# Linear attention: the decays of all six levels first, then all small products of a head and block in one go on TensorE

## The chip, the cores and the metric

The kernel runs on one core of a Trainium2 chip. The metric is the device time of one execution in microseconds (us). In the traces PE is TensorE (PEld its weight loads), ACT is ScalarE, DVE is VectorE, POOL is GpSimd and SP the engine that issues most DMAs.

## What is computed

Two layers act on 2064 tokens (16 learned ones ahead of 2048) of 1024 channels in float32. Layer 0 is a gated convolution module; the change does not touch it. Layer 1 is gated linear attention with four heads (keys and queries of 128 channels, values of 256), where every channel of a head decays by a gate of its own:

```python
def _gla_chunk_step(S, inp):
    qc, kc, vc, gc = inp
    bc = jnp.cumsum(gc, axis=1)
    o_inter = jnp.einsum('bthd,bhde->bthe', qc * jnp.exp(bc), S)
    diff = bc[:, :, None] - bc[:, None, :]
    decay = jnp.exp(jnp.where(causal[None, :, :, None, None], diff, -jnp.inf))
    att = jnp.einsum('bthd,bshd,btshd->bhts', qc, kc, decay)
    o_intra = jnp.einsum('bhts,bshe->bthe', att, vc)
    S_new = jnp.exp(b_last)[..., None] * S + jnp.einsum(
        'bshd,bshe->bhde', kc * jnp.exp(b_last[:, None] - bc), vc)
    return S_new, o_inter + o_intra
...
    o = o * lax.rsqrt(jnp.mean(o * o, axis=-1, keepdims=True) + RMS_EPS) * norm_g
    return (o * jax.nn.silu(r)) @ w_out
...
        h = layer_norm(DN_ALPHA * h + y, post_ln_g[i], post_ln_b[i])
```

## The kernel before

**Projections.** Layer 1 works on four blocks of 512 tokens (the first has the 16 learned ones besides). In each block `proj_units` projects, for head after head, the keys k, the queries q, the values v in four parts, and two gate tiles r0 and r1. A projection is a run of matmuls into a PSUM tile `pj`, each float32 product made of three passes over high and low parts (`mm3`: lines 105, 106 and 107 of the profile). All `pj` tiles share **three buffers** (the pool at L58): a fourth tile's first matmul waits until one of the three has been read out. Behind the keys comes one matmul z for the decay gates (L619), also into a `pj` tile, read by DVE (L620) and ACT (L621). Keys are read out by ACT at L599, queries at L601, the r tiles by ACT at L603 and DVE at L604. The SBUF tiles r0 and r1 have **one buffer each** (L593), so L603 for one head can only write when the head before has read its r (L777).

**Attention of a head** (`gla_units`, a generator of pieces, advanced by `phase3` in step with the projections of the next head: 2.35 pieces per projection). In order: the decayed keys are transposed on PE (pk, L677) and split by ACT and DVE into a pair k_h, k_l; `state(c)` makes the step of the state S for chunk c, three matmuls into `ds` that need that pair. Attention inside a chunk of 128 tokens is cut into six levels, of 64, 32, 16, 8, 4 and 2 tokens. For each level POOL takes differences of the summed gates b (L703, L704), ACT the exponential (L640), and DVE multiplies by keys and queries (L706, L707): this gives a tile A. Small matmuls multiply parts of A by other parts of it. The levels 64, 32 and 16 go to `att` at once, level by level (L713: 4, 8 and 16 matmuls). The levels 8, 4 and 2, and the products inside pairs (tile A1), go to the two tiles `sm` (L741, L742: 64 matmuls in all) behind the last level. DVE masks and sums them (L744 to L753) into `at`, ACT and POOL split that into a_h and a_l, and PE makes the output o of a chunk out of the states and of these (L105 to L107 again, six matmuls per chunk). Then o is squared (ACT L764), copied to SBUF (`osb`, DVE L765), scaled (DVE L767, POOL L768, DVE L770), transposed back (oT, PE L775) and multiplied by r (og, L777).

**PSUM.** Besides `pj` there are three buffers named g (transposes, `sm`, o, oT, and the transposed tokens of the next block, `trb`), and one each for `att` and `ds`: eight banks, all in use.

**Order.** The program is written as above; a list scheduler with its own timing model then sets the order of the instructions on each engine. So every engine's order is fixed in the program, and an instruction that waits holds up all that stand behind it on its engine.

Of the kernel before, what the change touches and what calls it, by code (L numbers as in the profile page):

```python
# [11 lines left out]
F32 = mybir.dt.float32  # L12
# [5 lines left out]
DRAM = bass.MemoryType.DRAM  # L18

P = 128  # L20
D = 1024
KD = D // P
T = 2064
# [9 lines left out]
ALPHA = math.sqrt(2.0)  # L33
# [15 lines left out]
class Trunk:  # L49
    """Two layers; float32 products as three float32r passes over exact high and low parts."""  # L50
# [34 lines left out]
    def load(self, srcs, nm, eng, parts=((0, KD),)):  # L85
        """[P, k, w] blocks from DRAM as (high, low) pairs per k; in turn with what `parts` yields."""
        out = []
        for i, src in enumerate(srcs):
            nk, w = src.shape[1:]
            r, h, l = (  # L90
                t[:, : nk * w].rearrange("p (k c) -> p k c", c=w)
                for t in (self.raw(f"{nm}_{i}"), *self.pair(f"{nm}_{i}"))
            )
            for k0, k1 in parts:
                ks = slice(k0, min(k1, nk))
                self.nc.sync.dma_start(r[:, ks], src[:, ks])
                self.split(r[:, ks], h[:, ks], l[:, ks], eng)
            out += [(h[:, k], l[:, k]) for k in range(nk)]
        return out

    def mm3(self, out, ops):
        """out = sum over (lhi, llo, rhi, rlo) of lhi*rhi + lhi*rlo + llo*rhi."""
        mm, n = self.nc.tensor.matmul, len(ops)
        for i, (lh, ll, rh, rl) in enumerate(ops):
            mm(out, lhsT=lh, rhs=rh, start=(i == 0), stop=False)  # L105
            mm(out, lhsT=lh, rhs=rl, start=False, stop=False)  # L106
            mm(out, lhsT=ll, rhs=rh, start=False, stop=(i == n - 1))  # L107
# [5 lines left out]

    def phase1(self, x_cm, w1, pp, c_d, sz_d, hook):
        nc = self.nc
# [5 lines left out]
        # what the last convolutions of the second segment use, apart from what closes earlier  # L121
        last = (KD - 1) % 3
# [31 lines left out]
        def first():  # L154
            """parts of the first weights, in turn with the first part of x"""
            load_x(0, (0, 1))
            yield 0, 2
            load_x(0, (1, 2))
            yield 2, 4
            load_x(0, (2, 4))  # L160
            yield 4, KD
# [104 lines left out]
        # the last gates: first the tokens that layer 0's next step starts with  # L266
# [17 lines left out]

    def phase2_open(self, pp, c_d, sz_d):
        """what may start while the last gates are projected"""
        nc = self.nc
        self.c_d, self.sz_d = c_d, sz_d
        self.lp = self.pool(self.st2, name="p2l", bufs=2, side="right")
        self.pm = [self.pool(self.st2, name="p2p", bufs=1, space=PSUM, side="right")]  # L290
        self.st2w = ExitStack()
        self.wrp = self.pool(self.st2w, name="p2r", bufs=WRB, side="right")
        self.prm2 = self.lp.tile([P, 16], F32, name="prm2", bufs=1)
        nc.sync.dma_start(self.prm2, pp)
        self.normed, self.gated, self.nnorm = deque(), deque(), 0
# [70 lines left out]
    def out_tile(self, h, l, w, xt, m, nm):  # L366
        """xt[:m] = ALPHA * xt[:m] + (h + l)^T w"""
        for e in range(2):
            es = slice(512 * e, 512 * (e + 1))
            ps = self.pjt(f"{nm}_{e}")[:m]  # L370
            self.mm3(ps, [(h[:, k], l[:, k], w[k][0][:, es], w[k][1][:, es]) for k in range(KD)])
            self.nc.vector.scalar_tensor_tensor(xt[:m, es], xt[:m, es], ALPHA, ps, op0=ALU.mult, op1=ALU.add)  # L372

    def ln_stats(self, sm, r, n, sfx):
        """mean and 1 / standard deviation (columns 0, 2) of the rows of r [n, D]"""
        nc = self.nc
        st = sm.tile([P, 2, 6], F32, tag="st", name=f"st{sfx}")
        rs = sm.tile([P, 4], F32, tag="rs", name=f"rs{sfx}")
        for i in range(2):
            nc.vector.bn_stats(st[:n, i], r[:n, 512 * i : 512 * (i + 1)])  # L380
        nc.vector.bn_aggr(rs[:n, 0:2], st[:n])
        nc.vector.tensor_scalar(rs[:n, 1:2], rs[:n, 1:2], LN_EPS, None, op0=ALU.add)  # L382
        nc.gpsimd.tensor_tensor(rs[:n, 2:3], rs[:n, 1:2], self.mhalf[:n, 0:1], op=ALU.pow)  # L383
        return rs

    def post_ln(self, sm, r, n, g, b, sfx):
        """LayerNorm over the free axis of r [n, D] (tokens on partitions)."""
# [46 lines left out]

    def phase3_open(self, ws):
        """what may start while layer 0 ends"""
# [15 lines left out]
    def phase3_init(self, wa2, pp, og_d):  # L452
# [11 lines left out]
        # w_a2 at rows 0, 32 (high parts) and 64 (low part)  # L464
# [10 lines left out]
    def block(self, bi):  # L475
        """h1 of a block of tokens, transposed and split; yields before each chunk of tokens"""
# [24 lines left out]
    def gla_consts(self, pool, tmp):  # L501
        nc, K = self.nc, self
        """Masks of the 32x32 diagonal blocks by level, block mask, chunk resets."""
# [13 lines left out]
        for lev, m in enumerate((8, 4, 2, 1, 0)):  # L517
            f = full
            nc.gpsimd.memset(f, 1.0)
            if m:  # L520
# [3 lines left out]
                # s (partition) in the first half of segment, t in the second half  # L524
# [6 lines left out]
            # the blocks on the diagonal, gathered into 32 columns  # L531
# [18 lines left out]
    def proj_units(self):  # L550
        """yields after each unit of PE work; weights of the next tile are loaded one tile ahead"""
# [3 lines left out]
        for i, (bi, (kind, h, _, wd)) in enumerate(jobs):  # L555
# [3 lines left out]
            # the meta tokens have no outputs: only keys, gates and values of theirs are needed  # L559
# [71 lines left out]
    def pair3(self, nm, x, eng, sfx, bufs=2):  # L631
        """x [P, 4, P] as (high, low)"""
        h, l = (self.gp.tile([P, 4, P], F32R, tag=f"{nm}_{i}", name=f"{nm}_{i}{sfx}", bufs=bufs) for i in "hl")
        self.split(x, h, l, eng)
        return h, l

    def gla_units(self, h, hd, bi, t0, n):
# [4 lines left out]
        if off:  # L642
            # meta tokens only enter the state
# [16 lines left out]
        # decays from and to the chunk's ends  # L660
# [17 lines left out]
        kth, ktl = self.pair3("k", pt, nc.vector, nm)  # L678
        Ss = []

        def state(c):
            """the state before chunk c, and its step"""
# [7 lines left out]
            self.mm3(ds, [(kth[:, c], ktl[:, c], vh[:, c], vl[:, c])])  # L690
# [3 lines left out]
        att = self.pa.tile([P, 4, P], F32, tag="att", name=f"att{nm}")  # L694
        nc.vector.memset(att, 0.0)
        lv = {}
        for m in (64, 32, 16, 8, 4, 2):
            A = self.gp.tile([P, 512], F32, tag="A", name=f"A{nm}_{m}", bufs=4)
            view = lambda x: x.rearrange("p (s u i) -> p s u i", u=2, i=m)
            Av, bv, kv, qv = view(A), view(bs), view(ks), view(qs)  # L700
            nsg = 512 // (2 * m)
            mid = bv[:, :, 0, m - 1 : m].to_broadcast([P, nsg, m])
# [6 lines left out]
            if m >= 16:  # L709
                for c in range(4):  # L710
                    for s in range(0, P, 2 * m):
                        a = c * P + s
                        nc.tensor.matmul(  # L713
                            att[s : s + m, c, s + m : s + 2 * m],
                            lhsT=A[:, a : a + m],
                            rhs=A[:, a + m : a + 2 * m],
                            start=False,
                            stop=False,
                            skip_group_check=True,
                        )  # L720
                state(len(Ss))
                yield
        # by blocks of 32: queries of odd rows, decayed to the row before, then all queries
# [6 lines left out]
        nc.gpsimd.tensor_copy(A1[:, :, 16:], qs.rearrange("p (a t) -> p a t", t=32))  # L730
        state(3)
        yield
        red = self.gp.tile([P, 4, 32], F32, tag="red", name=f"red{nm}")
        for c2 in range(2):
            sm = self.pt.tile([P, 2, 144], F32, tag="g", name=f"sm{nm}_{c2}")
            for c in range(2):
                for s in range(0, P, 32):
                    a = (2 * c2 + c) * P + s
                    w = slice(a, a + 32)
                    for i, m in enumerate((8, 4, 2)):  # L740
                        nc.tensor.matmul(sm[s : s + 32, c, 48 + 32 * i : 80 + 32 * i], lhsT=lv[m][:, w], rhs=lv[m][:, w], start=True, stop=True, skip_group_check=True)  # L741
                    nc.tensor.matmul(sm[s : s + 32, c, :48], lhsT=ks[:, w], rhs=A1[:, a // 32], start=True, stop=True, skip_group_check=True)  # L742
# [41 lines left out]
    def phase3(self, wo):  # L784
        """returns what is left of the last head, and half of layer 1's out-projection"""
# [20 lines left out]
    def load_half(self, wo, e, staging=None):  # L806
        """yields before each of four tiles"""
# [11 lines left out]

    def phase4(self, wo, rows, out):  # L820
# [3 lines left out]
        # the pair that the last projection reads, and the two others  # L824
# [114 lines left out]
```

## Time and profile before

| what | value |
|---|---|
| time, median of three runs (least, most) | 1764.78 us (1763.5, 1766.14) |
| span of the profiled execution | 1762.7 us |
| PE busy in it | 1705.0 us, 97% |
| PE weight loads | 1522.8 us, 86% |
| DVE, ACT, POOL busy | 79%, 48%, 53% |
| layer 1 without its out-projection, 829 to 1600 us: PE busy | 746.13 of 771 us |

The profiled execution's span lies 2.1 us under the median of the runs: that is what lies around the span. Busy PE is the total over the whole kernel; both layers are included. Names in the trace leave out numbers, in the order of a program they stand: `pj_b1k2_0` is the projection of block 1, keys, head 2; `o1_0_1` is block 1, head 0, second half of the tokens.

### The profile page before, as it was taken

To read this page: it belongs to the slowest core of one execution; us is meant where nothing else is said; L and a number is where in the kernel's file an instruction comes from. 1 tells how busy PE (TensorE), PEld (TensorE's weight loads), DVE (VectorE), ACT (ScalarE), POOL (GpSimd) and SP (SyncE) were. 2 spreads that over 40 slices of the span, in tenths; PEclk is the share of its full clock that TensorE was granted. 3 is DMA by queue.
4 is the path that set the end of the run, shared out by engine and by line. 5 is a ranking of instruction groups with operands and counts; after the bars stand their busy time and mean duration, and the time that the engine had idled before them with its cause. 6 is when DMAs were issued, how large, how long until landed. Compare 5 with 4: busy or idle time off the path is not lost.

```text
span 1762.7 us, 30279 instructions
## 1 busy us (share of the span) xinstructions
PE 1705.0 (97%) x12291; PEld 1522.8 (86%) x12291; DVE 1397.2 (79%) x1900; ACT 848.2 (48%) x1308; POOL 934.3 (53%) x675
## 2 busy tenths in 40 slices
PE   8999999999998999998999999999999999999998
PEld 8999999999997777777888888888888878888886
DVE  5799999999988888877676687787878697777665
ACT  6455565655635344445455454555555455541000
POOL 1889999999966687756233133333334153331000
PEclk9999999999998999999999999999999999999999
DMA  6111111211256444433113222232223322344441
GB/s 243 37 49 36 47 51 37 73 57 53 92 182 219 132 158 153 143 111 105 64 61 108 86 97 81 77 112 71 86 83 94 112 73 85 120 159 164 149 136 62
DMA packets 102492, 178.80 MB, mean 101 GB/s; under 512 B 8736, under 2 KB 64672, under 8 KB 102352
## 3 DMA queue, kind: packets, MB, share of 16 engines
q1 hardware_dynamic: 102352, 176.87, 30.4%
q8 instruction: 96, 1.57, 0.4%
q14 instruction: 44, 0.36, 0.1%
HBM read 134.70 MB, written 42.14 MB: 100 GB/s over the span
## 4 chain that ended last, share of the span: by engine, by line
PE 72%; DVE 14%; ACT 5%; POOL 4%; DMA 2%; issue 2%; SPq 0%; DVEq 0%; POOLq 0%; ACTq 0%
PE pj_y L107 5%; PE pj_y L106 5%; PE pj_y L105 5%; PE pj_g L106 3%; PE pj_g L107 3%; PE pj_a L106 3%; PE pj_z L106 3%; PE pj_z L107 3%; PE pj_z L105 3%; PE pj_a L105 3%; PE pj_g L105 3%; PE pj_a L107 3%; DVE A L707 2%; DVE A L706 2%; DMA c<-c_d 1%
## 5 line engine op out<-in xcount | busy, mean ns | idle before, releaser
L194 POOL TENSOR_TENSOR gacc<-gacc,prod 128x1024 f32<-128x1024 f32 (+1 forms) x156 | 384.5, 2468 | 60.1 <-ACT prod L193 51.2
L202 DVE SCALAR_TENSOR_TENSOR cacc<-glu,prm,cacc 128x1024 f32<-128x1024 f32 (+1 forms) x292 | 374.8, 1294 | 6.8
L703 POOL TENSOR_TENSOR A<-b 128x256 f32<-128x256 f32 x96 | 77.7, 809 | 304.8 <-DVE b L629 136.8
L193 ACT ACTIVATE prod<-glu,prm 128x1024 f32<-128x1024 f32 (+1 forms) x156 | 178.6, 1154 | 82.9 <-POOL gacc L194 82.7
L105 PE MATMUL pj_g<-xh,h_w 128*128 128x344 f32 x384 | 124.6, 324 | 5.3 <-ACT h_w L72 4.4
L106 PE MATMUL pj_g<-xl,h_w 128*128 128x344 f32 x384 | 124.6, 325 | 0.3 <-DVE xl L73 0.3
L107 PE MATMUL pj_g<-xh,l_w 128*128 128x344 f32 x384 | 123.7, 323 | 0.0
L106 PE MATMUL pj_a<-xl,h_w 128*128 128x344 f32 x384 | 123.1, 321 | 0.0
L105 PE MATMUL pj_z<-xh,h_w 128*128 128x344 f32 x384 | 123.1, 321 | 0.0
L106 PE MATMUL pj_z<-xl,h_w 128*128 128x344 f32 x384 | 123.0, 320 | 0.0
L105 PE MATMUL pj_a<-xh,h_w 128*128 128x344 f32 x384 | 123.0, 320 | 0.0
L107 PE MATMUL pj_z<-xh,l_w 128*128 128x344 f32 x384 | 122.8, 320 | 0.0
L107 PE MATMUL pj_a<-xh,l_w 128*128 128x344 f32 x384 | 122.7, 320 | 0.0
L106 PE MATMUL pj_y<-wol,h_gt 128*128 128x512 f32 (+1 forms) x272 | 110.2, 406 | 1.0 <-DVE wol L73 1.0
L107 PE MATMUL pj_y<-woh,l_gt 128*128 128x512 f32 (+1 forms) x272 | 109.2, 409 | 1.9 <-DVE l_gt L73 1.9
L105 PE MATMUL pj_y<-woh,h_gt 128*128 128x512 f32 (+1 forms) x272 | 110.8, 411 | 0.0
L105 PE MATMUL pj_y<-w4h,h_g 128*128 128x512 f32 x256 | 99.7, 390 | 0.0
L106 PE MATMUL pj_y<-w4l,h_g 128*128 128x512 f32 x256 | 99.6, 390 | 0.0
L107 PE MATMUL pj_y<-w4h,l_g 128*128 128x512 f32 x256 | 99.5, 389 | 0.0
L640 ACT ACTIVATE A<-A 128x512 f32<-128x512 f32 (+1 forms) x112 | 66.6, 596 | 52.9 <-POOL A L704 52.2
L383 POOL TENSOR_TENSOR rs<-rs,mhalf 128x1 f32<-128x1 f32 x16 | 14.5, 906 | 145.2 <-DVE rs L382 145.2
L372 DVE SCALAR_TENSOR_TENSOR xt<-xt,pj_y 128x512 f32<-128x512 f32 (+1 forms) x66 | 44.7, 680 | 58.8 <-PE pj_y L107 58.8
(420 smaller groups left out, 5474.6 us busy)
## 6 DMA issues: line engine op xcount, KB each, us to landing
r_w<-w SPq DMA_DIRECT2D x24, 512.0 KB, 3.5
sz_d<-sz SPq DMA_DIRECT2D x48, 172.0 KB, 1.9
c<-c_d SPq DMA_DIRECT2D x16, 512.0 KB, 5.1
szb<-sz_d SPq DMA_DIRECT2D x16, 512.0 KB, 5.0
xt<-x_tok SPq DMA_DIRECT2D x16, 512.0 KB, 3.7
h_d<-xt SPq DMA_DIRECT2D x16, 512.0 KB, 2.6
r_h1b<-h_d SPq DMA_DIRECT2D x16, 512.0 KB, 3.6
og_d<-og SPq DMA_DIRECT2D x32, 256.0 KB, 2.8
```

The source lines that it names most:

```text
L105: mm(out, lhsT=lh, rhs=rh, start=(i == 0), stop=False)
L106: mm(out, lhsT=lh, rhs=rl, start=False, stop=False)
L107: mm(out, lhsT=ll, rhs=rh, start=False, stop=(i == n - 1))
L193: nc.scalar.activation(pr, src(k), AF.Copy, scale=tap(k))
L194: nc.gpsimd.tensor_tensor(st["g"], st["g"], pr, op=ALU.add)
L202: nc.vector.scalar_tensor_tensor(out, src(k), tap(k), acc, op0=ALU.mult, op1=ALU.add)
L372: self.nc.vector.scalar_tensor_tensor(xt[:m, es], xt[:m, es], ALPHA, ps, op0=ALU.mult, op1=ALU.add)
L383: nc.gpsimd.tensor_tensor(rs[:n, 2:3], rs[:n, 1:2], self.mhalf[:n, 0:1], op=ALU.pow)
L640: ex = lambda o, i: nc.scalar.activation(o, i, AF.Exp, scale=1.0 / TAU)
L703: nc.gpsimd.tensor_tensor(Av[:, :, 0], mid, bv[:, :, 0], op=ALU.subtract)
L706: nc.vector.tensor_tensor(Av[:, :, 0], Av[:, :, 0], kv[:, :, 0], op=ALU.mult)
L707: nc.vector.tensor_tensor(Av[:, :, 1], Av[:, :, 1], qv[:, :, 1], op=ALU.mult)
```

## The change

Inside `gla_units` the six levels are made first, without any product: POOL, ACT and DVE work as before, in the order 64, 32, 16, 8, 4, 2, then A1. For that the tiles A get six buffers in place of four, and the transposed keys' pair one in place of two. The steps of the state stand between the levels and behind A1. All 92 small products of the head and block then come in one piece, which the scheduler is told to issue only after the last step of the state (`issue_after`): first the 64 products 32 wide, chunk by chunk, then the levels 16, 32 and 64. The piece that masks and sums follows. Nothing is computed otherwise; the rest of the difference is comments taken out, so lines behind stand up to six higher.

```diff
-        kth, ktl = self.pair3("k", pt, nc.vector, nm)
-        Ss = []
+        kth, ktl = self.pair3("k", pt, nc.vector, nm, 1)
+        Ss, steps = [], []
...
-            self.mm3(ds, [(kth[:, c], ktl[:, c], vh[:, c], vl[:, c])])
+            steps.append(self.mm3(ds, [(kth[:, c], ktl[:, c], vh[:, c], vl[:, c])]))
...
-        att = self.pa.tile([P, 4, P], F32, tag="att", name=f"att{nm}")
-        nc.vector.memset(att, 0.0)
-        for m in (64, 32, 16, 8, 4, 2):
-            A = self.gp.tile([P, 512], F32, tag="A", name=f"A{nm}_{m}", bufs=4)
+        def level(m):
+            A = self.gp.tile([P, 512], F32, tag="A", name=f"A{nm}_{m}", bufs=6)
...
+        for i, ms in enumerate(((64, 32), (16, 8), (4, 2))):
+            for m in ms:
+                level(m)
+            if i < 2:
                 state(len(Ss))
                 yield
...
+        state(2)
+        yield
+        att = self.pa.tile([P, 4, P], F32, tag="att", name=f"att{nm}")
+        nc.vector.memset(att, 0.0)
         state(3)
         yield
+        sms = [self.pt.tile([P, 2, 144], F32, tag="g", name=f"sm{nm}_{c2}") for c2 in range(2)]
+        part = partial(nc.tensor.matmul, skip_group_check=True)
+        with self.tc.issue_after(steps[-1].ins):
+            for c in range(4):
+                sm = sms[c // 2][:, c % 2]
+                for s in range(0, P, 32):
+                    w = slice(c * P + s, c * P + s + 32)
+                    part(sm[s : s + 32, :48], lhsT=ks[:, w], rhs=A1[:, (c * P + s) // 32], start=True, stop=True)
+                    for i, m in enumerate((8, 4, 2)):
+                        part(sm[s : s + 32, 48 + 32 * i : 80 + 32 * i], lhsT=lv[m][:, w], rhs=lv[m][:, w], start=True, stop=True)
+            for m in (16, 32, 64):
+                A = lv[m]
+                for c in range(4):
+                    for s in range(0, P, 2 * m):
+                        a = c * P + s
+                        part(att[s : s + m, c, s + m : s + 2 * m], lhsT=A[:, a : a + m], rhs=A[:, a + m : a + 2 * m], start=False, stop=False)
```

The scheduler orders layer 1 anew. Two places show how. The first is PE in block 1, between the end of the projections r of head 1 and the keys and queries of head 2, while the output of head 0 is finished. Before, in PE's order:

```order
L106 MATMUL pj_b1r11_0_10484<-xlb1_8834,h_b1r11_0_10401 128x512
L107 MATMUL pj_b1r11_0_10484<-xhb1_8833,l_b1r11_0_10402 128x512
...
L775 MATMUL oT1_0_1_10365<-ident_73,osb1_0_10228 128x128 x4
L677 MATMUL pk1_1_10447<-ident_73,kh1_1_10438 128x128 x4
L713 MATMUL att1_1_10456<-A1_1_16_10534 16x16 x15
L105 MATMUL pj_b1k2_0_10572<-xhb1_8833,h_b1k2_0_10478 128x512
L106 MATMUL pj_b1k2_0_10572<-xlb1_8834,h_b1k2_0_10478 128x512
```

After, at the same place:

```order
L107 MATMUL pj_b1k2_0_10565<-xhb1_8826,l_b1k2_0_10479 128x512
...
L107 MATMUL o1_0_1_10281<-vhb1v0_9451,a_l1_0_10225 128x256
L620 MATMUL pj_z1_2_0_10703<-ah1_9453,a2_7087 128x512
L105 MATMUL pj_b1q2_0_10738<-xhb1_8826,h_b1q2_0_10559 128x512
L106 MATMUL pj_b1q2_0_10738<-xlb1_8827,h_b1q2_0_10559 128x512
...
L105 MATMUL pj_b1q2_0_10738<-xhb1_8826,h_b1q2_0_10559 128x512
L781 MATMUL oT1_0_0_10330<-ident_73,osb1_0_10228 128x128 x4
L781 MATMUL oT1_0_1_10365<-ident_73,osb1_0_10228 128x128 x4
L678 MATMUL pk1_1_10447<-ident_73,kh1_1_10438 128x128 x4
L106 MATMUL pj_b1q2_0_10738<-xlb1_8827,h_b1q2_0_10559 128x512
```

Before, the transposes oT of head 0 and pk of head 1 stand ahead of the keys of head 2, with small products around them. After, they stand behind the keys, the gate product z and 19 matmuls of the queries of head 2.

The second excerpt is the same place on ACT. Before (L603 reads out r0 and r1 of head 1, L599 the keys of head 2, L621 the gate product):

```order
L603 ACTIVATE b1r01_10406<-pj_b1r01_0_10407 128x512
L72 ACTIVATE k_h1_1_10452<-pk1_1_10447 128x512
L603 ACTIVATE b1r11_10483<-pj_b1r11_0_10484 128x512
L72 ACTIVATE h_b1v2_1_10732<-r_b1v2_1_10731 128x1024
L599 ACTIVATE b1k2_10571<-pj_b1k2_0_10572 128x512
L72 ACTIVATE sh1_1_1_10525<-Sm1_8061 128x256
L621 ACTIVATE b1_2_10669<-pj_z1_2_0_10670,prm3_7082 128x512
```

After (the same are L604, L600 and L622):

```order
L600 ACTIVATE b1k2_10564<-pj_b1k2_0_10565 128x512
...
L641 ACTIVATE kh1_1_10438<-kh1_1_10438 128x512
L622 ACTIVATE b1_2_10702<-pj_z1_2_0_10703,prm3_7082 128x512
L623 ACTIVATE b1_2_10702<-b1_2_10702 128x512
L624 ACT_TABLE_LOAD
L624 ACTIVATE b1_2_10702<-b1_2_10702 128x512
L641 ACT_TABLE_LOAD
L641 ACTIVATE eb1_2_10970<-b1_2_10702 128x512
L604 ACTIVATE b1r01_10406<-pj_b1r01_0_10407 128x512
L72 ACTIVATE k_h1_1_10452<-pk1_1_10447 128x512
L604 ACTIVATE b1r11_10483<-pj_b1r11_0_10484 128x512
```

Before, ACT reads out both r tiles and then the keys. After, it reads out the keys and the gate product first and the r tiles behind them.

The third place is PE at the end of block 1, where the tokens of block 2 are transposed (`trb`) and head 2's output is made. Before:

```order
L107 MATMUL o1_2_1_11336<-vhb1v2_10804,a_l1_2_11315 128x256
L490 MATMUL trb2_256_0_11411<-ident_73,r_h1b2_256_11409 128x128 x4
L106 MATMUL pj_b1v3_3_11511<-l_b1v3_1_11277,xhb1_8833 128x256
L107 MATMUL pj_b1v3_3_11511<-h_b1v3_1_11276,xlb1_8834 128x256
L490 MATMUL trb2_256_1_11418<-ident_73,r_h1b2_256_11409 128x128 x4
L105 MATMUL pj_b1v3_3_11511<-h_b1v3_1_11276,xhb1_8833 128x256
...
L107 MATMUL pj_b1r03_0_11545<-xhb1_8833,l_b1r03_0_11370 128x512
L713 MATMUL att1_3_11634<-A1_3_64_11636 64x64 x2
L775 MATMUL oT1_2_0_11452<-ident_73,osb1_2_11318 128x128 x4
L490 MATMUL trb2_384_0_11462<-ident_73,r_h1b2_384_11460 128x128 x4
```

After:

```order
L746 MATMUL att1_2_11127<-A1_2_64_11026 64x64 x4
L491 MATMUL trb2_0_0_11255<-ident_73,r_h1b2_0_11253 128x128 x4
L491 MATMUL trb2_0_1_11262<-ident_73,r_h1b2_0_11253 128x128 x4
L105 MATMUL o1_2_0_11320<-sh1_2_0_11038,q_h1_2_10979 128x256
...
L107 MATMUL o1_2_1_11336<-sh1_2_2_11085,q_l1_2_10980 128x256
L105 MATMUL o1_2_0_11320<-vhb1v2_10804,a_h1_2_11314 128x256
...
L107 MATMUL o1_2_1_11336<-vhb1v2_10804,a_l1_2_11315 128x256
L491 MATMUL trb2_256_1_11418<-ident_73,r_h1b2_256_11409 128x128 x4
L781 MATMUL oT1_2_0_11452<-ident_73,osb1_2_11318 128x128
L491 MATMUL trb2_384_0_11462<-ident_73,r_h1b2_384_11460 128x128 x4
```

Before, the last o product of head 2 is followed by the rest of v3 and all of r0 of head 3 (24 matmuls), then oT. After, the 92 small products end in front of two transposed tiles and six o products, then come the o products that need a_h; and behind the last o product stand four transposes, then oT.

## Rows read from the trace of the kernel before

**Rows 1.** The page: span, and busy time and instructions of the engines.
```profile
span 1762.7 us, 30279 instructions
PE 1705.0 (97%) x12291; PEld 1522.8 (86%) x12291; DVE 1397.2 (79%) x1900; ACT 848.2 (48%) x1308; POOL 934.3 (53%) x675
```

**Rows 2.** Busy time by stretch, layer 1: us, engines, PEclk, DMA share, GB/s.
```profile
829.00:1600.00 771.00, 746.13 (x6946) 645.67 (x6945) 584.35 (x1025) 393.66 (x723) 262.55 (x284) 0.99 0.28 92
```

**Rows 3.** Timeline, PE: start, us, engine, line, out<-in, count; around one run of sm.
```profile
1245.10 0.28 PE L106 MATMUL ds<-vlb2v,k_h 128*128 128x256 f32 x1
1245.22 0.28 PE L107 MATMUL ds<-vhb2v,k_l 128*128 128x256 f32 x1
1245.43 0.26 PE L741 MATMUL sm<-A 128*32 128x32 f32 x4
...
1247.05 0.25 PE L742 MATMUL sm<-A,b2k 128*32 128x48 f32 x2
1247.23 0.50 PE L106 MATMUL pj_b2q<-xlb,h_b2q 128*128 128x512 f32 x1
1247.57 0.40 PE L107 MATMUL pj_b2q<-xhb,l_b2q 128*128 128x512 f32 x1
1247.81 0.39 PE L105 MATMUL pj_b2q<-xhb,h_b2q 128*128 128x512 f32 x1
```

**Rows 4.** Timeline, PE: the first and the last of 103 runs of small products.
```profile
830.62 0.33 PE L713 MATMUL att<-A 128*64 128x64 f32 x2
...
1585.53 0.25 PE L742 MATMUL sm<-A,b3k 128*32 128x48 f32 x2
```

**Rows 5.** Timeline, all engines: from a last o product to the second r evacuated.
```profile
1082.59 0.28 PE L107 MATMUL o<-vhb1v,a_l 128*128 128x256 f32 x1
...
1083.63 0.68 DVE L765 COPY osb<-o 128x512 f32<-128x512 f32 x1
...
1087.18 1.14 DVE L770 TENSOR_SCALAR osb<-osb,sq 128x256 f32<-128x256 f32 x4
...
1090.31 0.60 PE L677 MATMUL pk<-ident,kh 128*128 128x128 f32 x4
...
1091.74 0.59 ACT L72 ACTIVATE k_h<-pk 128x512 fp32r<-128x512 f32 x1
1091.88 0.74 DVE L777 SCALAR_TENSOR_TENSOR og<-oT,prm,b1r 128x512 f32<-128x512 f32 x1
...
1092.65 0.60 ACT L603 ACTIVATE b1r<-pj_b1r 128x512 f32<-128x512 f32 x1 [0.33 <-DVE og L777]
```

**Rows 6.** Timeline: the last sm product of a head, and its a_h.
```profile
1203.18 0.25 PE L742 MATMUL sm<-A,b1k 128*32 128x48 f32 x2
...
1207.11 0.63 ACT L72 ACTIVATE a_h<-at 128x512 fp32r<-128x512 f32 x1 [0.22 <-DVE at L753]
...
1207.88 1.93 POOL L73 TENSOR_TENSOR a_l<-at,a_h 128x512 fp32r<-128x512 f32 x1 [17.03 <-ACT a_h L72]
```

**Rows 7.** Waits of PE by releaser: us in total, times, longest.
```profile
PE pj_b0q L105 <- ACT b0k L599: 1.0, 1, 1.0
```

**Rows 8.** Timeline: a gate product z and its two readers.
```profile
1051.62 0.50 PE L619 MATMUL pj_z<-ah,a 128*128 128x512 f32 x1
...
1053.43 0.74 DVE L620 TENSOR_SCALAR gl<-pj_z,prm 128x512 f32<-128x512 f32 x1
...
1054.20 0.69 ACT L621 ACTIVATE b<-pj_z,prm 128x512 f32<-128x512 f32 x1 [3.06 <-DVE gl L620]
```

**Rows 9.** Timeline: a wait of PE (in brackets, with its releaser).
```profile
836.13 0.68 PE L677 MATMUL pk<-ident,kh 128*128 128x128 f32 x4 [3.38 <-DVE kh L671]
```

**Rows 10.** Busy time by stretch, behind that wait (columns as rows 2).
```profile
836.70:840.00 3.30, 3.30 (x17) 3.30 (x17) 3.04 (x6) 1.26 (x3) 0.00 (x0) 0.50 0.70 236
840.00:843.00 3.00, 3.00 (x63) 2.49 (x63) 0.48 (x1) 0.82 (x3) 1.19 (x2) 0.99 0.08 33
```

**Rows 11.** The page's costliest groups: first decay difference of a level, on POOL.
```profile
L703 POOL TENSOR_TENSOR A<-b 128x256 f32<-128x256 f32 x96 | 77.7, 809 | 304.8 <-DVE b L629 136.8
```

More of the change, by code (lines that the diff above doesn't have):

```diff
@@ L106, in mm3 @@
             mm(out, lhsT=lh, rhs=rl, start=False, stop=False)
-            mm(out, lhsT=ll, rhs=rh, start=False, stop=(i == n - 1))
+            end = mm(out, lhsT=ll, rhs=rh, start=False, stop=(i == n - 1))
+        return end
     def pjt(self, nm):
@@ L689, in state @@
             ds = self.pa.tile([P, 4, P], F32, tag="ds", name=f"ds{nm}_{c}").rearrange("p a b -> p (a b)")[:, :256]
-            self.mm3(ds, [(kth[:, c], ktl[:, c], vh[:, c], vl[:, c])])
+            steps.append(self.mm3(ds, [(kth[:, c], ktl[:, c], vh[:, c], vl[:, c])]))
             nc.vector.scalar_tensor_tensor(S, S, el[:, c], ds, op0=ALU.mult, op1=ALU.add)
         yield
-        att = self.pa.tile([P, 4, P], F32, tag="att", name=f"att{nm}")
-        nc.vector.memset(att, 0.0)
         lv = {}
-        for m in (64, 32, 16, 8, 4, 2):
-            A = self.gp.tile([P, 512], F32, tag="A", name=f"A{nm}_{m}", bufs=4)
+        def level(m):
+            A = self.gp.tile([P, 512], F32, tag="A", name=f"A{nm}_{m}", bufs=6)
             view = lambda x: x.rearrange("p (s u i) -> p s u i", u=2, i=m)
             Av, bv, kv, qv = view(A), view(bs), view(ks), view(qs)
-            nsg = 512 // (2 * m)
-            mid = bv[:, :, 0, m - 1 : m].to_broadcast([P, nsg, m])
+            mid = bv[:, :, 0, m - 1 : m].to_broadcast([P, 512 // (2 * m), m])
             nc.gpsimd.tensor_tensor(Av[:, :, 0], mid, bv[:, :, 0], op=ALU.subtract)
@@ L708, in gla_units @@
             lv[m] = A
[L709 to L720, printed above, removed]
+        for i, ms in enumerate(((64, 32), (16, 8), (4, 2))):
+            for m in ms:
+                level(m)
+            if i < 2:
                 state(len(Ss))
@@ L730, in gla_units @@
         nc.gpsimd.tensor_copy(A1[:, :, 16:], qs.rearrange("p (a t) -> p a t", t=32))
+        state(2)
+        yield
+        att = self.pa.tile([P, 4, P], F32, tag="att", name=f"att{nm}")
+        nc.vector.memset(att, 0.0)
         state(3)
         yield
-        red = self.gp.tile([P, 4, 32], F32, tag="red", name=f"red{nm}")
[L734 to L742, printed above, removed]
+        sms = [self.pt.tile([P, 2, 144], F32, tag="g", name=f"sm{nm}_{c2}") for c2 in range(2)]
[14 more added lines that the diff above has]
+                        part(att[s : s + m, c, s + m : s + 2 * m], lhsT=A[:, a : a + m], rhs=A[:, a + m : a + 2 * m], start=False, stop=False)
+        red = self.gp.tile([P, 4, 32], F32, tag="red", name=f"red{nm}")
+        for c2, sm in enumerate(sms):
             ms = self.gp.tile([P, 2, 144], F32, tag="ms", name=f"ms{nm}_{c2}")
```

## The prediction, made before the changed kernel ran

> **What bounds the kernel now.** I read the page first: PE is busy 1705.0 of 1762.7 us, and its instructions run in an order that the program fixes [rows 1]. So the time is PE's own work plus its waits, and the change has to be costed in both. Then the stretch that it touches: in layer 1, from 829 to 1600 us, PE is busy 746.13 of 771 us, which leaves 24.9 us without work [rows 2]. Up to there both programs have the same order. The list of PE's waits shows what is short when PE does wait on a projection tile: the queries of block 0 waited 1.0 us once for the keys to be read out of PSUM [rows 7]. The timeline shows in what company the small products run: in **103 runs**, from 830.62 to 1585.53 us, most of them cut into by projections [rows 4]. In the order of the changed program they are 16 runs of 92. So the change does what it says, and "it changes nothing" is no rival.
>
> **1. The switches saved.** Around one run [rows 3]: two full-width matmuls of 256 columns start 0.12 us apart (1245.10, 1245.22), but the first small one comes 0.21 after the second, so going in costs 0.09. The last small matmuls start at 1247.05 (a row of two) and the projection at 1247.23. By the starts of such rows the small ones need about 0.02 each, so some 0.14 of the 0.18 is not work, against 0.02 inside the run: 0.12. The projection's next matmul starts 0.34 later (1247.57) where the one after needs 0.24 (1247.81): 0.10. Together **0.31 us per run**. 103 − 16 = 87 runs fewer make 27.0 us. Against that each of the 16 pieces switches once inside itself, from products 32 wide to wider ones; I take the way in, 0.09, for that: 16 × 0.09 = 1.4. Gain 27.0 − 1.4 = **−26 us**. Bounds: if the way out costs half as much elsewhere, (0.09 + 0.11) × 87 = −18; if the way in also slows the next step by 0.10, as the way out does, 0.41 × 87 = −36.
>
> The Trainium skill, "TensorEngine Tiling (Array Packing)", Key Properties, says that a change of the tiling mode drains TensorE, and gives no price. By that rule the switch inside a piece is a full one, 16 × 0.31 = 5 us, and the gain 22; rows 3 agree that a switch costs something. The sum does not use it.
>
> **2. What the new order puts in front of the r tiles.** This is the term that decides. An r tile leaves its `pj` buffer only when og of the head before has read the old r, since r0 and r1 have one SBUF buffer each. The way there is long: the last o product ends at 1082.87, the copy of o starts at 1083.63, the scaling ends at 1088.32, and the second r is read out at 1092.65 to 1093.25, released by og [rows 5]: 10.4 us. Before, PE's order is r0, r1, oT, pk, then the next keys, and ACT reads out r0, r1, then keys. After, PE's order is r0, r1, keys, the last o products, z, 19 matmuls of the queries, and only then oT. While oT is not done, two of the three `pj` buffers hold r tiles. The keys take the third; z must wait until ACT has read out the keys, and the queries until DVE and ACT have read z. Nothing stands between them on PE but what waits too. What that costs: the keys' read-out, 0 to 1.0 us (1.0 in [rows 7]; the six o products in between, at 0.12, can cover 0.7); z's, from its start at 1051.62 to the end of ACT's read at 1054.89, 3.27 us less the 0.25 that z takes itself, so 3.0 with a loaded DVE [rows 8]; with an idle one 0.50 + 0.1 + 0.74 + 0.69 = 2.0, less 0.25, or somewhat less where matmuls overlap, 1.6. So each place costs 1.6 to 4.0; I take 3.5, near the loaded row, since DVE is behind with levels and splits at that point. Going through the order head by head I count six places of z and queries in front of oT (heads 2 and 3 of blocks 1, 2 and 3) and three of the same kind with other projections (two in block 0, and a tile of the out-projection in front of the oT of block 3's head 2): 9 × 3.5 = **+31 us** (14 to 36).
>
> **3. The ends of blocks 0, 1 and 2.** At these three places the last head's products meet the transposes of the next block, and no projection stands between. From the last 32-wide product (end 1203.43) to a_h (end 1207.74) DVE and ACT need 4.3 us [rows 6]. PE has 28 products of `att` in between (about 1.0 us by the pace of rows 3, 48 products in 1.7), eight transposes at 0.60 per four [rows 5] and six o products of 0.12: 2.7 us, so it waits 1.6. From the last o product to the first scaled part of `osb` it takes 4.6 us, to all four 5.45 [rows 5], and there are four to twelve transposes in front of oT, of which the later ones need a PSUM buffer g that o still holds until its copy is done (1083.63 + 0.68, that is 1.4 us after the last o): 3.5 to 4.4 of wait, and about 1 us each at two transposed tiles. Together 1.6 + 4.4 + 2 = **8 us, three times: +24** (5.4 each without the two waits for g, so 16; 12 each if a_l, 1.93 us of POOL behind a_h in [rows 6], is waited for too, so 36). Before, the rest of v and all of r0, some 8 us of PE work, lay in that gap.
>
> **4. The transposed keys.** In five heads (1_2, 2_0, 2_1, 2_2, 3_0) pk is followed within 0.3 to 0.4 us of PE work by the first step of the state, which needs k_h. From the end of pk (1090.91) to that of k_h (1092.33) it is 1.4 us [rows 5]. Before, 2 to 6 us of projection lay in between. 5 × 1.1 = 5.5, with a queue on ACT now and then **+6** (0 where ACT's other reads also shift the pair earlier, 13 where DVE's k_l is late too). The single buffer of the pair costs nothing: the last step of the state of one head stands long before pk of the next.
>
> **5. The clock.** Behind a wait of 3.38 us [rows 9] the granted clock was 0.50, the lower of the two levels (1.2 GHz), for the stretch from 836.70 to 840.00; behind that it was 0.99 [rows 10]. At half speed 3.3 us hold 1.65 us of work, so such a wait costs 1.65 more. Of the 9 + 6 longer waits above I let ten do that: 10 × 1.65 = **+17** (0 to 20).
>
> The Trainium skill, "TensorE: Matmul & The Clock Gate", HAM oscillation, describes the same: an engine that waits again and again starts cold each time. By that all 15 would pay, +25 in place of +17, and the time would be 1825; rows 9 and 10 show one such case here, and cannot say how many.
>
> **6. The rest.** Levels, exponentials and masks are as many as before, on engines with 47 to 79% of use or less; six buffers of A in place of four hold POOL's next levels back until a piece is done, which is rival C. The `issue_after` itself adds an order on PE, no instruction.
>
> **Sum.** −26 + 31 + 24 + 6 + 17 = +52. Against the profiled span 1762.7 + 52 = 1814.7; the median of the runs lies 2.1 above the span, so **1817 us**. All low ends together (gain 36, then 14, 16, 0, 0) give −6: 1759. All high ends (gain 18, then 36, 36, 13, 20) give +87: 1852.
>
> **Rivals.**
> - **A, faster.** The waits of parts 2 to 4 are hidden and only the switches remain: 1764.8 − 26 = **1739**. The place is z: if ACT read out keys and z as soon as PE ends them, and DVE is idle when z comes, z costs less than 1 us. It decides where all new waits together stay under 26 us, that is 1.6 us per head. For it speaks that the order was made by a scheduler that had these dependencies before it; against it, that the r tiles hold two of three buffers whatever DVE does, and that 3.0 us is the row's duration, of which 1.6 cannot be hidden.
> - **B, it cancels.** Waits at their low ends and no new falls of the clock: −26 + 14 + 16 + 0 = +4, so about **1769** (1760 to 1776).
> - **C, POOL.** In the changed order a_l of a head stands on POOL behind the level work of the next head: twelve differences at 0.81 us [rows 11] and a copy, some 10.5 us, which cannot start before the piece is through, since all six A are in use. If o's products with a_l then wait 3 us in 13 of 16 heads, 39 more: 1817 + 39 = **1856**. Against it: in most heads two or more projections stand between the piece and those products.
>
> **How the numbers follow.** Chances: the forecast (parts 2 to 5 within their bounds, 1776 to 1850) 0.70; B 0.10; A 0.13; C 0.07. A difference of 0.2%, 3.5 us, is about what a measurement of this kernel tells from none. B splits evenly between within 0.2% (up to 1768.3) and slower. So faster 0.13, within 0.2% 0.05, slower 0.70 + 0.07 + 0.05 = 0.82. The range for 8 in 10 leaves out A and half of C and of the lowest part of B: 1764 to 1852.
>
> **What would show it.** Runs: PE's timeline should show 16 pieces; next to a piece the steps 0.21 and 0.34 of rows 3, and nothing of the kind elsewhere. PE's busy time from 829 to the end of layer 1's heads should fall by about 26 us less what the lower clock adds. Part 2: in the list of waits, projections of queries waiting for ACT's or DVE's read of z, and z for ACT's read of the keys, some 30 us where there was 1.0; L604 waiting for og. Part 3: oT waiting for `osb` and o for a_h, 3 times 6 us or more, at the ends of blocks 0, 1, 2. Part 4: ds waiting for k_h. Part 5: stretches of granted clock 0.50 behind these waits. I am wrong if z's readers come at once, or if the pieces themselves run slower than their parts did, since 92 products wait for one another's PSUM tile; then PE's busy time would rise and not its waits.

## The result, and the profile after

The changed kernel takes 1855.46 us (1852.01 to 1857.23, four runs) against 1764.7 before (four runs): a ratio of **1.0512** (95% interval 1.05 to 1.0525), so 90.8 us slower. The sign and most places were forecast; the size, 1817 with a range up to 1852, was too small.

The page after, its span and busy time (against [rows 1]), and the stretch of layer 1 to the end by the windows view (columns as in [rows 2]; the last row is the same stretch of the kernel before):

```profile
span 1855.3 us, 30235 instructions
PE 1729.4 (93%) x12291; PEld 1548.0 (83%) x12291; DVE 1409.3 (76%) x1900; ACT 850.1 (46%) x1308; POOL 913.7 (49%) x675
829.00:1855.30 1026.30, 925.88 (x7637) 799.44 (x7635) 698.95 (x1194) 409.97 (x740) 256.56 (x300) 0.94 0.27 90
829.00:1762.70 933.70, 900.87 (x7637) 773.77 (x7635) 685.09 (x1194) 407.76 (x740) 277.06 (x300) 0.99 0.30 99
```

The 92.6 us by which this execution's span is longer split in three. PE without work: 1026.30 − 925.88 = 100.4 against 32.8, **+67.6**. Half clock: going through the trace, from 829 us to the end of PE's work the granted clock was 0.50 in 17 stretches, 116 us in all, with PE busy for 87.4 of them; before, in three stretches of 3.4 us, with PE busy throughout. Half of 87.4 less half of 10.2 is **+38.6**. The rest is 92.6 − 67.6 − 38.6 = **−13.6**, the switches saved, less small things.

The waits of PE after, by releaser (us in total, times, longest):

```profile
PE oT L781 <- DVE osb L776: 9.8, 5, 3.1
PE o L105 <- DVE xlb L494: 7.9, 3, 3.5
PE pj_z L620 <- ACT b3k L600: 6.6, 2, 5.9
PE pj_z L620 <- ACT b2k L600: 5.9, 2, 5.2
PE trb L491 <- DVE xlb L494: 5.8, 3, 4.6
PE ds L105 <- ACT k_h L72: 5.5, 5, 1.5
PE o L105 <- ACT kh L770: 4.9, 6, 1.8
PE pj_z L620 <- ACT b1k L600: 4.9, 2, 4.2
...
PE pj_b3q L105 <- ACT b L622: 4.1, 2, 2.6
PE pj_b1q L105 <- ACT b L622: 3.8, 2, 2.6
```

Before, z waited for nothing, queries had the one row of [rows 7], and ds did not wait for k_h; the other waits named here had these rows:

```profile
PE oT L775 <- DVE osb L770: 2.5, 4, 1.5
PE o L105 <- DVE xlb L493: 2.1, 1, 2.1
PE trb L490 <- DVE xlb L493: 2.0, 2, 1.0
PE o L105 <- ACT kh L764: 1.5, 2, 0.8
```

Read them by place. z waits for the keys' read-out (L600), queries for z's (L622): part 2. oT for `osb`, and o and trb for a PSUM buffer that token transposes hold (xlb): part 3. ds for k_h: part 4. The row of o for kh (L770) is a wait for the square of the chunk before, which ACT writes into the tile kh; the prediction had no part for it.

One piece of small products, PE's timeline (against [rows 3]): the way in (0.21 between the starts, 0.09 of it extra) and the second step behind (0.22, 0.10 of it extra) cost what they did, and all 92 products, two records each, lie between.

```profile
1304.37 0.28 PE L107 MATMUL ds<-vhb2v,k_l 128*128 128x256 f32 x1
1304.58 0.27 PE L738 MATMUL sm<-A,b2k 128*32 128x48 f32 x2
...
1308.72 0.39 PE L105 MATMUL o<-sh,q_h 128*128 128x256 f32 x1
1308.94 0.28 PE L106 MATMUL o<-sl,q_h 128*128 128x256 f32 x1
1309.06 0.28 PE L107 MATMUL o<-sh,q_l 128*128 128x256 f32 x1
```

The longest kind of wait, at z of the last head of block 2. First ACT's timeline (in brackets the idle time before and who ended it):

```profile
1379.44 1.06 ACT L72 ACTIVATE h_b2v<-r_b2v 128x1024 fp32r<-128x1024 f32 x1 [7.49 <-DMA r_b2v<-wv]
1380.41 0.36 ACT L770 ACTIVATE kh<-o 128x256 f32<-128x256 f32 x1
...
1385.52 1.06 ACT L72 ACTIVATE h_b2v<-r_b2v 128x1024 fp32r<-128x1024 f32 x1 [4.66 <-DMA r_b2v<-wv]
1386.48 0.58 ACT L600 ACTIVATE b2k<-pj_b2k 128x512 f32<-128x512 f32 x1
```

Then SP's queue (the issues of transfers):

```profile
1359.03 0.33 SPq L486 DMA_DIRECT2D r_h1b<-h_d  x1
1374.17 0.33 SPq L96 DMA_DIRECT2D r_b2v<-wv  x1
...
1381.79 0.33 SPq L96 DMA_DIRECT2D r_b2v<-wv  x1
```

And PE:

```profile
1381.61 0.28 PE L107 MATMUL o<-vhb2v,a_l 128*128 128x256 f32 x1
1387.11 0.80 PE L620 MATMUL pj_z<-ah,a 128*128 128x512 f32 x1 [5.23 <-ACT b2k L600]
1387.98 0.58 PE L105 MATMUL o<-sh,q_h 128*128 128x256 f32 x1
...
1390.84 0.80 PE L105 MATMUL pj_b2q<-xhb,h_b2q 128*128 128x512 f32 x1 [1.20 <-ACT b L622]
```

The tokens of the next block (r_h1b) took one of two staging buffers at 1359, and the weights of the values had to share the other: the second half was issued at 1381.79, when DVE had read the first. ACT stood in front of its split for 4.66 us, and **behind it in ACT's queue** stood the read-out of the keys, for which z waited. (The 5.86 us at the last z of block 3 have the same shape: there ACT stood 4.41 us for a weight transfer of the out-projection.) In the stretch that follows, the windows view shows half clock:

```profile
1382.20:1395.80 13.60, 7.41 (x19) 5.54 (x20) 7.15 (x12) 7.87 (x14) 2.05 (x2) 0.50 0.23 77
```

### The profile page after: what moved, and what is told of

It is laid out like the page before. It is cut to its first block, busy times and chain, and to the rows that moved or that the text cites. A ratio compares the mean times of both kernels' runs of the same rounds, so it can differ in the third digit from the quotient of the medians.

```text
span 1855.3 us, 30235 instructions
## 1 busy us (share of the span) xinstructions
PE 1729.4 (93%) x12291; PEld 1548.0 (83%) x12291; DVE 1409.3 (76%) x1900; ACT 850.1 (46%) x1308; POOL 913.7 (49%) x675
## 3 DMA queue, kind: packets, MB, share of 16 engines
q1 hardware_dynamic: 102352, 176.87, 28.2%
## 4 chain that ended last, share of the span: by engine, by line
PE 72%; DVE 12%; POOL 6%; ACT 4%; DMA 4%; issue 3%; SPq 0%; DVEq 0%; ACTq 0%; POOLq 0%
PE pj_y L107 4%; PE pj_y L105 4%; PE pj_y L106 4%; PE pj_g L106 3%; PE pj_a L106 3%; PE pj_g L107 3%; PE pj_z L107 3%; PE pj_z L106 3%; PE pj_a L105 3%; PE pj_a L107 3%; PE pj_z L105 3%; PE pj_g L105 3%; PE sm L740 2%; DMA c<-c_d 1%; DVE A L707 1%
## 5 line engine op out<-in xcount | busy, mean ns | idle before, releaser
L73 POOL TENSOR_TENSOR q_l<-eb,q_h 128x512 fp32r<-128x512 f32 x16 | 21.5, 1347 | 172.6 <-ACT q_h L72 172.6
```

The lines of the kernel that those rows point to most:

```text
L73: eng.tensor_tensor(lo, raw, hi, op=ALU.subtract)
```

## The experiments

Theory P is the prediction's part 2 (r tiles hold two of three projection buffers until og of the head before). Theory W came out of the rows above (a late weight transfer holds up ACT's queue). e1 to e11 are one run each and are compared with the run of the kernel before beside them, 1763.6 to 1767.8 us. Every edit lets the scheduler order layer 1 anew, so a run shows what an edit does together with its new order.

**e1, two buffers for r** (and the room for them).

```diff
-                t = hd[kind] = self.hp.tile([P, BMAX], F32, tag=kind, name=f"{nm}", bufs=2 if kind in "kq" else 1)
+                t = hd[kind] = self.hp.tile([P, BMAX], F32, tag=kind, name=f"{nm}", bufs=2)
```

> The changed kernel with two SBUF buffers for each of the tiles r0 and r1 (room from tiles that one engine alone uses, and from tokens of blocks 1 and 3). Theory P (projection tiles r hold two of three PSUM buffers until og of the head before): r can be read out at once, so z and the queries find a free buffer. In the profile of the changed kernel PE waits 20 us at z for the keys' or r's read-out and 10 us at queries for z's; both should fall under 5 in all, with some 15 us of the half clock behind them: 1855 - 25 - 15 = about 1815. Rival W (ACT stands at a weight split whose transfer is late, and the keys' read-out stands behind it): the r tiles are read out on the same ACT, so at least the three longest waits, 15 us, stay: about 1840.

Measured 1816.41. All waits of z and of queries for z's readers are gone from the list, whose head is now

```profile
PE oT L781 <- DVE osb L776: 14.2, 7, 3.5
PE o L105 <- ACT kh L770: 7.5, 10, 1.4
PE o L105 <- ACT a_h L72: 7.1, 3, 3.4
```

So P holds, the longest waits included: with a third `pj` buffer free, a late read-out of the keys stops nothing. oT does not stand earlier in e1's order (in block 1 it stands behind z and most or all of the queries, at two heads behind most of the values as well), so it is the second r buffer and not an earlier oT that frees z. PE's time without work fell by 23.8 us, and what the half clock takes by 10.8.

**e2, z in another PSUM bank.**

```diff
-  ps = self.pjt(f"z{bi}_{h}_{c0}")[:, :m]
+  ps = self.pa.tile([P, 4, P], F32, tag="att", name=f"z{bi}_{h}_{c0}").rearrange("p a b -> p (a b)")[:, :m]
```

> The changed kernel with the gate product z in the PSUM bank of att instead of one of the three projection buffers. Theory P: z waits for nothing of the projections, and queries only for the keys' read-out: the 10 us of queries that wait for z go, and of z's 20 us most: about 1820. Rival W: the keys' read-out is late by itself, so the three longest waits (4.2, 5.2, 5.9 us) move from z to the queries; only the 10 us go, and about 5 us of clock: about 1840.

Measured 1865.31: slower, against both. The waits moved: queries wait for the keys' read-out, and oT, in the new order, for `osb`:

```profile
PE oT L781 <- DVE osb L776: 36.4, 8, 8.8
PE pj_b2q L105 <- ACT b2k L600: 12.7, 3, 4.5
PE pj_b1q L105 <- ACT b1k L600: 8.0, 2, 4.1
```

With two r tiles in PSUM the queries are short of a buffer as z was; but the scheduler made another order, so the run tells nothing about sizes, and neither forecast can be weighed by it.

**e3, the tokens in a buffer of their own** (with the same room made), and **e4, e2 and e3 together.**

```diff
-  h1 = self.raw(f"h1{nm}_{o}")[:, :D]
+  h1 = self.hp.tile([P, D], F32, tag="h1", name=f"r_h1{nm}_{o}", bufs=1) if bi else self.raw(f"h1{nm}_{o}")[:, :D]
```

> The changed kernel with a buffer of its own for the tokens of the next block, so that both staging buffers stay with the weights. Theory P: no change at z and at the queries, 1850 to 1857. Rival W: the transfer of the values' second half is issued one split earlier; the three waits of 4.2 to 5.9 us at z fall to about 1 us, and the half clock behind them: 1855 - 12 - 8 = about 1835.

> The changed kernel with z in att's bank and the tokens in a buffer of their own. If P and W are both at work, what e2 and e3 give adds up: about 1815. If P alone, as e2; if W alone, as e3.

Measured 1827.93 and 1867.51. e3: z's waits for the keys of blocks 1 and 2 fell from 4.9 and 5.9 to 1.5 and 1.4 us, for block 3, where no tokens follow, 6.6 became 6.7. The rows of e3:

```profile
PE pj_z L620 <- ACT b3k L600: 6.7, 3, 4.5
PE pj_z L620 <- ACT b1k L600: 1.5, 2, 0.8
PE pj_z L620 <- ACT b2k L600: 1.4, 2, 0.7
```

W is at work in two of three places. The whole gain, 27.5 us, is more than these 7.9 us and their clock, so part of it comes from elsewhere in the new order. e4 takes what e2 takes, and nothing adds up.

**e8, control: the room alone.** Tiles that only DVE touches (`ms`, `red`), and the learned tokens' values, with one buffer; token tiles of 512 columns for blocks 1 and 3.

> Control for e1 and e3: the changed kernel with only the room made that they need (one buffer in place of two for tiles that DVE alone uses and for the learned tokens' values, smaller token tiles for blocks 1 and 3), and nothing put into it. If e1 and e3 owe their times to the second r buffer and to the tokens' own buffer, this is 1850 to 1862; if to the new order that the scheduler makes of any edit, it is as much faster as they, 1815 to 1830.

Measured 1856.65: e1 and e3 owe their times to the buffers, with the orders that these allow, and not to the room made for them.

**e5, not held back; e6, held back to the first step** (the two pieces of the diff)**; e7, the kernel before with its 64 products 32 wide in one piece behind `issue_after(steps[-1].ins)`.**

```diff
-        with self.tc.issue_after(steps[-1].ins):
+        if True:
...
-        with self.tc.issue_after(steps[-1].ins):
+        with self.tc.issue_after(steps[0].ins):
```

> The changed kernel without the order that holds the 92 products back until the last step of the state: the levels are still made first and the products still written in one piece, but the scheduler places them when their levels are ready (59 runs in its order, none behind the last step by rule). Theory L (the harm comes from holding the products back: everything behind them, from the masks to oT, starts late and oT is late for the r tiles): the waits of PE in layer 1 come back to 25 to 35 us, few falls of the clock, and the gain of 44 runs fewer than before shows, 44 x 0.31 = 14 us: 1750 to 1770. Rival M (the harm comes from making the levels first: six buffers A, long stretches of POOL and DVE ahead of everything else): waits stay near 90 us, 1830 to 1855.

> The changed kernel with the products held back until the first step of the state in place of the last (48 runs). Theory L: as e5, 55 runs fewer than before are worth 17 us: 1748 to 1768. Rival M: 1830 to 1855. Rival G (products that come in long runs of up to 77 hold up the engine that reads them): between, by the number of runs, about 1800.

> The kernel before with one part of the change alone: its 64 products 32 wide come in one piece behind the last step of the state, while the levels and the products of levels 64, 32 and 16 stay where they were (62 runs). Theory L: although 41 runs fewer save 13 us, the output of each head starts late: PE waits 60 to 90 us in layer 1 and the clock falls some ten times: 1805 to 1835. Rival M: 13 us faster than before, about 1752.

Measured 1777.62, 1774.73 and 1815.32. Holding the products back until the last step, and not at all or until the first, costs 78 and 81 us of the 91; it costs 50 in a kernel that is otherwise the one before (e12 below joins these 64 products too, holds nothing back and loses nothing). In e7 it is not z that waits most:

```profile
PE oT L778 <- DVE osb L773: 11.6, 8, 3.1
PE ds L107 <- DVE k_l L73: 9.0, 6, 2.2
```

Levels first (M) is not the main harm, yet e5 and e6 are still 12 and 9 us slower than before, and above L's ranges, where fewer runs of small products should make them faster. M and G explain none of the large difference.

**e9, the squares behind both chunks; e10, the same edit in the kernel before.** Each output tile holds two chunks; the second chunk's products had been written behind the square (ACT L770) of the first.

```diff
                 self.mm3(o, [(qh[:, c], ql[:, c], *Ss[c]), (ath[:, c], atl[:, c], vh[:, c], vl[:, c])])
-                nc.scalar.activation(junk, o, AF.Square, accum_out=sq[:, 0, c : c + 1])
+            for c in (2 * c2, 2 * c2 + 1):
+                nc.scalar.activation(junk, o2[:, c % 2], AF.Square, accum_out=sq[:, 0, c : c + 1])
```

> The changed kernel, held back until the last step as it is, but both chunks of an output tile are multiplied before ACT squares either (before, the second chunk's products waited for the square of the first, which stands on ACT behind weight splits that wait for transfers). In the changed kernel PE waited 4.9 us there by name, and the two waits of 4 to 6 us at z had that square in the same queue. Theory L: holding back remains, at most 5 to 20 us better: 1835 to 1850. Rival Q (it is ACT's queue, with the squares in it, that makes z, queries and oT late): waits fall by half, clock with them: 1795 to 1815.

> The kernel before with the same edit of the squares. PE waits 1.5 us for a square there, so by every theory 1762 to 1767.

Measured 1789.98 and 1768.77. e9 has the 16 pieces and the late start, and 65 us less, more than even Q forecast. So L as I had put it falls: being late is not enough. The squares matter, as Q said. How they do so I read from PE's order, which no run held fixed while it moved the squares alone; here from r0 of head 1 to oT of head 0 in block 1, tile by tile with the count of matmuls:

```
before  r01 x24, small, o_1 x6, small, r11 x24, small, oT x8
after   r01 x24, r11 x11, o_0 o_1 x2, r11 x13, k2 x8, o_0 x6, k2 x16, o_1 x6, z x1, q2 x19, oT x8
e9      r01 x24, r11 x10, o_0 x7, o_1 x7, r11 x14, k2 x22, oT x8
```

In the changed kernel the second chunks' products stand 8 and 24 matmuls into the keys, where the scheduler places each behind a square on a full ACT. So oT comes to stand behind z and 19 matmuls of the queries, where the r tiles hold the buffers. With the squares behind, oT stands ahead of z again, and z's waits come to 1.5 us in all, the longest of them this:

```profile
PE pj_z L620 <- ACT b1k L600: 0.5, 1, 0.5
```

In the kernel before the same edit gains nothing (+0.3% in one run).

**e11, the two edits and the tokens' buffer with the first step.**

> What the runs point to as the better version: levels first, products held back until the first step only, squares behind both chunks, tokens in their own buffer. e6 lost 10 us at the squares and 6 at the tokens' transposes: without these 1774.7 - 16 = 1758, some 7 us faster than before; if the waits move to the next place in the queue, 1770 to 1775.

Measured 1769.05 beside 1763.61, slower than forecast. The waits at squares are gone and those at the tokens' transposes are 2.1 us, but v and r projections now wait for DVE to read v out (some 22 us in the list).

**e12, e13: fewer runs without levels first.** Levels in three steps, products of 64, 32 and 16 behind the first, all 64 products 32 wide written in one piece, nothing held back (`level` as in the change but with four buffers A as before, `prods` the products of `att`); e13 adds e9's edit.

```diff
-        for m in (64, 32, 16, 8, 4, 2):
...
+        for ms in ((64, 32, 16), (8, 4), (2,)):
+            for m in ms:
+                level(m)
+            prods([m for m in ms if m >= 16])
+            state(len(Ss))
+            yield
```

> The kernel before with fewer runs and nothing held back: the levels in three steps (64, 32 and 16; 8 and 4; 2) with the products of 64, 32 and 16 behind the first, and all 64 products 32 wide written in one piece (76 runs in its order, 103 before). If what e5 and e6 lose comes from six levels made in one stretch (DVE's level products beside POOL's work, so that v and r projections wait for DVE), this one keeps the switches' gain, 27 x 0.35 = 9 us: 1754 to 1759. If it comes from any new order that joins products, 1768 to 1780.

> e12 with the squares behind both chunks of an output tile (73 runs). Where squares in ACT's queue hold up o's products, 3 to 8 us faster than e12; as e10 against before, up to 5 us slower.

e12 took 1762.62 (ten runs), ratio 0.9991 (0.9981 to 1.0), between its two forecasts; e13 took **1753.74, ratio 0.9938 (0.9923 to 0.9953)** (four runs): 11 us faster than the kernel before, 9 us faster than e12, and the fastest of all. From 829 us on its PE is busy for 894.93 of 923.10:

```profile
829.00:1752.10 923.10, 894.93 (x7639) 776.32 (x7637) 689.15 (x1195) 405.18 (x741) 278.17 (x300) 0.99 0.30 100
```

That is 28.2 us without work (32.8 before) and 5.9 us less PE time, with 73 runs.

## Why the prediction was right or wrong

**Part 1, switches: −26 forecast, −28 measured, then partly lost.** Over all runs of small products the steps in, out and behind, read from the starts, cost 37.9 us before (0.37 per run) and 5.3 after, −32.6. Inside, a piece at full clock takes 3.99 us, so 63.8 for 16, where the same products took 59.1: +4.7. What the sum had no term for is the restart: from 829 us on PE stops 73 times where it stopped 25 times, and each time the starts around the gap lie 0.2 to 0.3 us further apart than gap and pace explain. By this estimate 48 more stops take 10 to 14 us, about what lies between −28 and the −13.6 that remain.

**Part 2, z and queries: +31 forecast.** The rows of z, queries and the r tiles' read-outs add up to some 35 us, ACT's read-out of r stood 8.0 us for og in block 2 as forecast, and e1 shows the mechanism. The split was wrong: z's wait for the keys was set at 0 to 1.0 by the one row of before, and was 4.2, 5.2 and 5.9 at the last heads, as ACT's queue stood at a weight transfer (e3). Queries waited about 10 where the sum held more. The sum came near because the two errors offset each other.

**Part 3, block ends: +24 forecast.** oT for `osb` 9.8, o and trb for xlb 13.7: 23.5. That this meets the sum is luck too: only 6.2 of the 9.8 lie at block ends (two waits like the one below), no wait for a_h shows where the sum had 4.8, and the waits for a PSUM buffer were 13.7 where it had 6.

```profile
1222.97 0.45 PE L781 MATMUL oT<-ident,osb 128*128 128x128 f32 x1 [3.11 <-DVE osb L776]
```

**Part 4: +6 forecast,** 5.5 for k_h and 2.6 for k_l. All that PE's idle time grew by, +67.6, stands against 31 + 24 + 6 = 61.

**Part 5, the clock, is the step that failed: +17 forecast, +38.6 measured.** I took ten falls of one stretch of 3.4 us each. There were 17 stretches, 14 more than before, and ten of the 17 lasted 6.8 to 13.7 us. In seven of these ten a further wait began while the clock was still down, as in the row at 1382, which holds the end of one wait and a second of 1.20 us; in the other three the clock was down before the wait had ended. So what failed is that I priced waits one by one, and gave each the half clock of one short stretch. The rule of the Trainium skill that stood beside this part ("TensorE: Matmul & The Clock Gate", HAM oscillation), by which every such wait pays, gave +25: nearer than my choice and still too low. Of the five terms this one and the switches left their bounds: 38.6 against 0 to 20, and a gain of 13.6 against 18 to 36.

Between the +52 of the sum and the +92.6 of this execution lie 40.6 us: 21.6 of the clock, 12.4 of the switches' gain, most of it taken back by the restarts, and 6.6 of waits. Rivals A and B fell with the waits. C's time came out, but not its mechanism: no wait of o for a_l is among those of 0.2 us or more.

Some of the sum's own figures do not follow from its terms. The switches' low end is 0.20 × 87 = 17, and 16 with the switch inside a piece, not 18; part 3's high end is three times 8 + 1.93, 30 and not 36, and the work in its gap is 1.0 + 1.2 + 0.7 = 2.9 and not 2.7; part 5's high end is 15 × 1.65 = 25 and not 20; ACT's share in [rows 1] is 48% and not 47. Put right, all high ends make +88 in place of +87, so the measured time lies outside either way.

**What set it off** I had not seen: two things together, each in the order that the scheduler makes with it. With the products held back and the squares between an output tile's chunks, 91 us; held back without those squares, 26 (e9); with the squares but held back only to the first step, 9 (e6); the kernel before, with its 64 products alone held back, 50 (e7). e7 with the squares behind was not run.

**Still open** is the last 10 us of e5 and e6. That DVE's level products beside POOL's work are the cause fits the rows below and e11's waits for DVE, and was not tried by itself; PE's own list in e6 has squares (10.2 us) and `osb` (7.1) at its head, and e11, without the waits for squares, is 4 us nearer to the kernel before. Open too is why e2's order made `osb` so late.

## What to carry to other kernels

Before joining small operations to save switches, ask what they were waiting for and what waits for them: a piece that starts at the last of its inputs starts everything behind it late, and here what stood behind it decided whether that cost 26 or 91 us. Where a few PSUM buffers are read out by an engine in order, list what can stand at that engine's queue (a transfer, a square, a tile still being read), since any of it can stop TensorE at the next tile. Price a row of waits with the clock that they take down, and by the sum of half-clock stretches, not by their number.

## What the runs showed of the hardware

DVE's level products, 256 columns in float32, took 0.41 us where POOL did nothing and 0.83 where POOL worked through them (medians in the changed kernel: 85 and 97 of 192). Beside POOL's a_l, of 1.47 us, one took 1.51. DVE and POOL in the changed kernel:

```profile
1369.99 0.82 DVE L707 TENSOR_TENSOR A<-A,b2q 128x256 f32<-128x256 f32 x1
1370.74 0.83 DVE L706 TENSOR_TENSOR A<-A,b2k 128x256 f32<-128x256 f32 x1
1371.50 1.51 DVE L707 TENSOR_TENSOR A<-A,b2q 128x256 f32<-128x256 f32 x1
1372.93 1.22 DVE L73 TENSOR_TENSOR l_b2q<-r_b2q,h_b2q 128x1024 fp32r<-128x1024 f32 x1
1374.06 0.41 DVE L706 TENSOR_TENSOR A<-A,b2k 128x256 f32<-128x256 f32 x1
...
1370.50 0.79 POOL L704 TENSOR_TENSOR A<-b 128x256 f32<-128x256 f32 x1
1371.25 1.47 POOL L73 TENSOR_TENSOR a_l<-at,a_h 128x512 fp32r<-128x512 f32 x1
```

POOL is busy to 1372.7 here; by the rows DVE's next level product takes 0.41 again.

In e6, 155 of the 192 lay wholly beside POOL's work, before 81: by the two medians some 74 × 0.42 = 31 us more of DVE's time in layer 1, an estimate.
